# The output projection of a mixer block, split by the rows of its weight: one half computed among the latent projections

## The chip, the cores and the metric

The kernel runs on one core of a Trainium2 chip. The metric is device time in microseconds (us) for one execution of the whole kernel; the kernel before took 1762.07 us, the median of three runs (1761.93 to 1762.74). PE is the matrix engine (TensorE), DVE the vector engine, ACT the scalar engine, POOL the GpSimd engine, and SP the engine on which nearly all loads are issued. SBUF is the on-chip memory, PSUM the accumulators that PE writes.

## The reference, cut to what matters

One layer on a sequence of 1024 tokens with 1024 features, in float32:

```
x = x + 1/2 * SwiGLU_1(RMSNorm(x))
h = RMSNorm(x) @ W_in            -> u (512) | v (512) | c_q (256) | c_kv (128) | k_rope (32)
y_A = gelu(u) * (masked W_s @ RMSNorm(gelu(v)) + b)          # gMLP, 512 wide
q = rmsnorm(c_q) @ w_uq ; k, v = rmsnorm(c_kv) @ w_ukv       # the latents; per-head norms, rotary
y_B = block-causal attention(q, k, v)                         # 8 heads, 512 wide
x = x + concat(RMSNorm(y_A), RMSNorm(y_B)) @ W_out            # W_out is 1024 x 1024
x = x + 1/2 * SwiGLU_2(RMSNorm(x))
x = RMSNorm(x)
```

RMSNorm(y_A) and RMSNorm(y_B) are separate norms, so the product with W_out is a sum of two: the gMLP half times the first 512 rows of W_out, and the attention half times the last 512 rows.

## The kernel before

**Tiles.** The 1024 tokens are eight row tiles t of 128. Every float32 product is made of three matmuls on values that are split into a high and a low part: high times high, high times low, low times high. A split is a copy on ACT (the high part, L291) and a subtraction on DVE (the low part, also L291); for the rows of W_out the copy `woh` is on ACT (L1123) and the subtraction `wol` on POOL (L1124).

**Stages, in the order of time.** FFN 1 with gate and up, then down (0 to 650 us), which leaves x in the DRAM tensor `x1d`; v, u and the gMLP (640 to 762 us); the latents (762 to about 860 us); attention (820 to 1010 us); the way out, that is the product with W_out (1011 to 1112 us); FFN 2 (1112 to 1757 us), whose gate and up products are called GU below.

**What sets the order.** The program is a list of `Step` objects, run in order; `before(lead, fn)` puts a piece of work that many steps ahead of a step, and `do` appends a piece. A string of steps such as "a0 c0 a1 k0 l0" names them. A scheduler then reorders instructions on each engine by its own model, and a planner gives each tile its place in SBUF, so that a tile that takes over the place of another has to wait for the last user of that one. DVE, ACT, POOL and SP each work through their instructions in order.

**The steps that matter.** `a` (`latent_in`) multiplies x by the last 416 columns of W_in; `c` (`latent_T`) transposes its result and splits it into `chl`; `l` (`latent_tile`) makes q, k and v of one row tile (L917 to L926 on PE), then on DVE the squares' sums, an inverse square root by three Newton rounds of three small instructions each (L280 to L282), and two scalings (L955, L956), and on POOL the rotary part (L816 to L820, L958). `x` (`attend`) is one stage of attention on one item, a head and a pair of row tiles: head transposes (`head_T`, L973), scores (L988 to L990), softmax (L992, L994), transposed probabilities (L1017), weighted sums (L1026, L1027), the fold (L1038, L1040). The items are taken heads 0 to 2 first, and five stages of attention lie among the last latents.

**The way out.** `gmlp_pair` makes the normed gMLP half `ya` and stores it in the DRAM tensor `yAd`. The eight 128-row pieces of W_out are loaded and split by `load_out` at the end of attention, two pieces to each of the last four items. `y_tile` loads the gMLP half back, norms the attention half beside it, transposes the eight 128x128 blocks and splits them. `out_tile` runs 48 matmuls of 512 columns (eight pieces, two halves of the columns, three products), adds x1 to the two banks (L1163), stores the sum in `x2d`, and makes the normed and transposed operand of FFN 2 (`xo2.tile`: the norm L305, transposes L300, sums and splits L386 to L408). The first weights of GU (`raw_b`, 512 KB for each load) are loaded at the leads of `load_at`.

Of the kernel before, what the change touches and what calls it, by code (L numbers as in the profile page):

```python
# [11 lines left out]
F32R = mybir.dt.float32r  # L12
# [222 lines left out]
def block(nc, x, positions, ffn1_norm, ffn1_w_gate, ffn1_w_up,  # L235
# [71 lines left out]
    def rows(t):  # L307
        return slice(t * P, (t + 1) * P)
# [328 lines left out]
    yAd = nc.dram([S, GW], "yAd")  # L637
# [248 lines left out]
    def gmlp_pair(p):  # L886
        u, ps = mx["u"][p], mx.pop(("mix", p))
        for g in range(4):
            gs = slice(g * P, (g + 1) * P)
            nc.vector.scalar_tensor_tensor(u[:, :, gs], ps[:, g], bT[:, g:g + 1], u[:, :, gs],  # L890
                                           op0=ALU.add, op1=ALU.mult)
        for j in range(2):
            t = 2 * p + j
            ya = tile_([P, GW], f"ya{t}")
            r = row_rstd(u[:, j, :], ya, f"ya{t}", GW)
            nc.vector.scalar_tensor_tensor(ya, u[:, j, :], r, mx["goA"], op0=ALU.mult, op1=ALU.mult)
            nc.gpsimd.dma_start(yAd[rows(t), :], ya)
# [145 lines left out]
    items = [(h, pi) for ps in ((0, 1), (2, 3)) for h in range(3) for pi in ps]  # L1043
    items += [(h, pi) for h in range(3, H) for pi in range(NT // 2)]
# [5 lines left out]
    def attend(n):  # L1050
# [66 lines left out]
    def load_out(k):
        hi = tile_([P, D], f"woh{k}", F32R)
        lo = tile_([P, D], f"wol{k}", F32R)
        for e in range(2):  # L1120
            es = slice(e * 512, (e + 1) * 512)
            raw = load(tile_([P, 512], f"raw_wo{k}_{e}"), wov[:, k, es])
            nc.scalar.copy(hi[:, es], raw)  # L1123
            nc.gpsimd.tensor_tensor(lo[:, es], raw, f(hi[:, es]), op=ALU.subtract)  # L1124
        wo[k] = (hi, lo)
# [8 lines left out]
    def y_tile(t):  # L1134
        y = tile_([P, D], f"y{t}")
        load(y[:, 0:GW], yAd[rows(t), :])
        ysrc = mx["yB"][t // 4][:, t % 4].rearrange("p h d -> p (h d)")
        r = row_rstd(ysrc, y[:, GW:], f"yb{t}", GW)
        nc.vector.scalar_tensor_tensor(y[:, GW:], ysrc, r, mx["goB"], op0=ALU.mult, op1=ALU.mult)
        hv = transposed(y, f"y{t}")  # L1140
        yh = tile_([P, KD, P], f"yh{t}", F32R)
        yl = tile_([P, KD, P], f"yl{t}", F32R)
        for k in range(2):
            split(hv[k], yh[:, 4 * k:4 * k + 4, :], yl[:, 4 * k:4 * k + 4, :])
        mx["y", t] = (yh, yl)
# [3 lines left out]
    def out_tile(t):  # L1149
        x2 = row_tile(x1d[rows(t), :], f"x2_{t}")  # L1150
        yh, yl = mx["y", t]
        pe = [bank(f"wo{t}_{e}") for e in range(2)]
        for k in range(KD):
            wh, wl = wo[k]
            for e in range(2):
                es = slice(e * 512, (e + 1) * 512)
                mm(pe[e], yh[:, k, :], wh[:, es], start=k == 0, stop=False)  # L1157
                mm(pe[e], yh[:, k, :], wl[:, es], start=False, stop=False)  # L1158
            for e in range(2):
                mm(pe[e], yl[:, k, :], wh[:, e * 512:(e + 1) * 512], start=False, stop=k == KD - 1)  # L1160
        for e in range(2):
            es = slice(e * 512, (e + 1) * 512)
            nc.vector.tensor_tensor(x2[:, es], pe[e], x2[:, es], op=ALU.add)  # L1163
# [8 lines left out]
    for t in range(2, NT):  # L1172
        ws_[t].before(1, lambda t=t: y_tile(t), ws_[0].index)
# [3 lines left out]
    gu2.steps(GU_ORDER, base2 - 1, load_at={(0, 0): base2 - 2, (0, 1): base2 - 1, (1, 0): base2, (1, 1): base2,  # L1177
# [63 lines left out]
```

## Time and profile before

| | us |
|---|---|
| median of three runs | 1762.07 |
| the profiled execution, its own time | 1762.42 |
| its span in the trace | 1760.6 |
| PE busy | 1716.5 (97%) |
| DVE busy | 1132.8 (64%) |
| ACT busy | 740.3 (42%) |
| POOL busy | 151.5 (9%) |
| chain of work that ended last: PE, DVE, ACT, DMA | 90%, 4%, 3%, 2% |

The span is 1.8 us shorter than the profiled execution's own time, and that execution is 0.35 us over the median. Busy PE includes time at the lower clock, so a busy share of 97% does not mean that 97% of the time is needed: the granted clock (1.00 is 2.4 GHz, 0.50 is 1.2 GHz) has to be read beside it. A matmul's printed duration is longer than its share of the engine, since matmuls are pipelined; what one costs is the distance of two starts.

### The profile page before, as it was taken

To read this page: it belongs to the slowest core of one execution; us is meant where nothing else is said; L and a number is where in the kernel's file an instruction comes from. 1 tells how busy PE (TensorE), PEld (TensorE's weight loads), DVE (VectorE), ACT (ScalarE), POOL (GpSimd) and SP (SyncE) were. 2 spreads that over 40 slices of the span, in tenths; PEclk is the share of its full clock that TensorE was granted. 3 is DMA by queue.
4 is the path that set the end of the run, shared out by engine and by line. 5 is a ranking of instruction groups with operands and counts; after the bars stand their busy time and mean duration, and the time that the engine had idled before them with its cause. 6 is when DMAs were issued, how large, how long until landed. Compare 5 with 4: busy or idle time off the path is not lost.

```text
span 1760.6 us, 21281 instructions
## 1 busy us (share of the span) xinstructions
PE 1716.5 (97%) x8196; PEld 1446.7 (82%) x8196; DVE 1132.8 (64%) x1597; ACT 740.3 (42%) x1125; POOL 151.5 (9%) x288
## 2 busy tenths in 40 slices
PE   8999999999999999999799999999999999999997
PEld 7788888888888888898699888778888888888886
DVE  7965656555578567469777644675665555648774
ACT  6533333334324344346577823443333333433442
POOL 1100000000000004333200511000000000000010
PEclk9999999999999999999799999999999999999999
DMA  7043232325835521200000422413322231693431
GB/s 257 12 144 120 90 120 90 112 74 195 313 125 186 167 85 48 94 25 1 1 1 1 158 88 97 161 54 112 127 102 90 96 118 70 210 345 107 161 126 48
DMA packets 122981, 199.51 MB, mean 113 GB/s; under 512 B 11008, under 2 KB 57600, under 8 KB 122880
## 3 DMA queue, kind: packets, MB, share of 16 engines
q1 hardware_dynamic: 118784, 184.52, 31.1%
q0 software_dynamic: 3520, 12.58, 1.8%
q8 instruction: 64, 1.05, 0.2%
q10 hardware_dynamic: 576, 1.05, 0.2%
q14 instruction: 37, 0.30, 0.1%
HBM read 143.07 MB, written 55.05 MB: 113 GB/s over the span
## 4 chain that ended last, share of the span: by engine, by line
PE 90%; DVE 4%; ACT 3%; DMA 2%; issue 1%; POOL 0%; SPq 0%; POOLq 0%; ACTq 0%; DVEq 0%
PE psum L468 46%; PE psum L597 8%; PE psum L599 8%; PE psum L600 8%; PE psum L744 2%; PE psum L745 2%; PE psum L746 2%; PE psum L1160 2%; PE psum L1157 2%; PE psum L1158 2%; PE psum L1017 2%; PE psum L300 1%; PE psum L1027 1%; PE psum L1026 1%; PE psum L988 1%; PE psum L990 1%
## 5 line engine op out<-in xcount | busy, mean ns | idle before, releaser
L483 DVE TENSOR_TENSOR P_a<-psum,P_a 128x1024 f32<-128x1024 f32 x33 | 40.3, 1222 | 80.1 <-PE psum L468 80.1
L483 DVE TENSOR_TENSOR P_b<-psum,P_b 128x1024 f32<-128x1024 f32 x33 | 40.3, 1222 | 59.4 <-PE psum L468 59.4
L473 ACT COPY P_b<-psum 128x1024 f32<-128x1024 f32 x33 | 33.5, 1014 | 77.3 <-PE psum L468 77.3
L473 ACT COPY P_a<-psum 128x1024 f32<-128x1024 f32 x33 | 33.5, 1016 | 73.4 <-PE psum L468 73.4
L484 ACT ACTIVATE P_a<-P_a 128x512 f32<-128x512 f32 x33 | 20.9, 633 | 102.7 <-DVE P_a L483 102.6
L271 POOL TENSOR_TENSOR r_fin<-ms_fin,mhalf 128x1 f32<-128x1 f32 x8 | 7.0, 876 | 610.7 <-DVE ms_fin L269 610.7
L291 DVE TENSOR_TENSOR pl<-psum,ph 128x512 fp32r<-128x512 f32 (+1 forms) x80 | 48.5, 629 | 14.1 <-ACT ph L291 14.1
L992 DVE TENSOR_REDUCE nm<-psum 128x1 f32<-128x128 f32 (+3 forms) x64 | 47.0, 751 | 12.9 <-PE psum L990 12.8
L725 POOL DMA_DIRECT2D x1d<-x_a x8 | 4.6, 580 | 569.9 <-DVE x_a L611 568.3
L994 ACT ACTIVATE p<-psum,nm 128x128 f32<-128x128 f32 (+3 forms) x64 | 47.8, 752 | 12.9 <-DVE nm L992 11.7
L484 ACT ACTIVATE P_b<-P_b 128x512 f32<-128x512 f32 x33 | 20.8, 631 | 76.6 <-DVE P_b L483 76.4
L1157 PE MATMUL psum<-woh,yh 128*128 128x512 f32 x128 | 51.2, 400 | 0.0
L1158 PE MATMUL psum<-wol,yh 128*128 128x512 f32 x128 | 49.9, 390 | 0.0
L1017 PE MATMUL psum<-ident,p 128*128 128x128 f32 x288 | 44.2, 285 | 4.9 <-ACT p L994 4.9
L1027 PE MATMUL psum<-pl,vv 128*128 128x256 f32 x160 | 43.7, 299 | 3.2 <-DVE pl L291 3.2
L1160 PE MATMUL psum<-woh,yl 128*128 128x512 f32 x128 | 45.2, 392 | 0.0
L1026 PE MATMUL psum<-ph,vv 128*128 128x256 f32 x160 | 43.9, 298 | 1.3 <-ACT ph L291 1.3
L291 ACT CAST ph<-psum 128x512 fp32r<-128x512 f32 (+1 forms) x80 | 41.4, 559 | 8.5 <-PE psum L1017 6.6
L988 PE MATMUL psum<-kh,qh 128*128 128x512 f32 (+2 forms) x96 | 38.6, 406 | 3.7 <-ACT kn L940 3.5
L1017 PEld LDWEIGHTS psum<-ident,p 128*128 128x128 f32 x288 | 35.0, 148 | 7.7 <-ACT p L994 5.9
L611 DVE SCALAR_TENSOR_TENSOR x_b<-psum,x_b 128x512 f32<-128x512 f32 x32 | 21.0, 685 | 27.0 <-PE psum L600 27.0
L1027 PEld LDWEIGHTS psum<-pl,vv 128*128 128x128 f32 x160 | 31.3, 196 | 4.9 <-DVE pl L291 3.6
(525 smaller groups left out, 5256.9 us busy)
## 6 DMA issues: line engine op xcount, KB each, us to landing
raw_a<-in_ffn_w_gate SPq DMA_DIRECT2D x22, 512.0 KB, 4.3
raw_a<-in_ffn_w_up SPq DMA_DIRECT2D x22, 512.0 KB, 5.7
hd<-hS_a SPq DMA_DIRECT2D x44, 256.0 KB, 2.2
raw_b<-in_ffn_w_gate SPq DMA_DIRECT2D x22, 512.0 KB, 4.1
raw_b<-in_ffn_w_up SPq DMA_DIRECT2D x22, 512.0 KB, 5.1
hd<-hS_b SPq DMA_DIRECT2D x44, 256.0 KB, 2.2
wB_a<-in_ffn_w_down SPq DMA_DIRECT2D x20, 512.0 KB, 5.3
aS_a<-hd SPq DMA_DIRECT2D x20, 512.0 KB, 3.7
```

The source lines that it names most:

```text
L291: return nc.scalar.copy(hi, src), nc.vector.tensor_tensor(lo, src, f(hi), op=ALU.subtract)
L468: mm(bk[:, m * 512:(m + 1) * 512], lhs[:, 4 * m + k, :], rhs[:, k, :], start=pn in FIRST and n == k == 0, stop=n == 2 and k == 3, skip_gro ...
L473: nc.scalar.copy(ev[u, pn], bk)
L483: nc.vector.tensor_tensor(c, bk, c, op=ALU.add)
L597: mm(banks[t], hh[:, j, tl], dh[:, j, :], start=pn in DOWN_FIRST and c == 0 and j == 0, stop=False, skip_group_check=True)
L599: mm(banks[t], hh[:, j, tl], dl[:, j, :], start=False, stop=False, skip_group_check=True)
L600: mm(banks[t], hl[:, j, tl], dh[:, j, :], start=False, stop=c == 5, skip_group_check=True)
L1017: nc.tensor.transpose(ps[:, i * P:(i + 1) * P], prs[j][:, c * P:(c + 1) * P], ident)
L1027: mm(acc[:, 0:256], mx["vv"][c][:, h, :], lo, start=False, stop=i == len(pts) - 1)
L1157: mm(pe[e], yh[:, k, :], wh[:, es], start=k == 0, stop=False)
L1158: mm(pe[e], yh[:, k, :], wl[:, es], start=False, stop=False)
L1160: mm(pe[e], yl[:, k, :], wh[:, e * 512:(e + 1) * 512], start=False, stop=k == KD - 1)
```

## The change

**What it does.** The product with W_out is taken apart by rows. `out_half(t, half, src)` multiplies one half: 24 matmuls (four pieces of W_out, two column halves, three products), and adds `src` to the banks. The gMLP half of row tile t is a step `o` of its own (`out_a`), which adds x1 and stores the sum in a new DRAM tensor `x15d`; its transposes and split (`y_a`) come one step ahead. The eight steps o0 to o7 stand among the steps l4 to l7 and the first three stages of attention. `ya` stays in SBUF until it is transposed there, so `yAd` with its eight stores and loads is gone. Four pieces of W_out are loaded and split eight, six, four and two steps ahead of o0, the other four at the last two items of attention. `out_tile` computes the attention half alone and adds `x15d`, not x1.

**What else moves with it.** The steps `a` come earlier and the steps `l` later. Three stages of attention lie among the latents, not five; the first items are those of heads 0 and 1 only, and the transposes of head 2 are made where those of the other heads are. `y_tile(t)` runs two steps ahead of its `out_tile`, not one, and the first weights of GU are due one to two steps earlier, in steps that are now half as long.

```diff
-            nc.gpsimd.dma_start(yAd[rows(t), :], ya)
+            mx["ya", t] = ya
...
-    items = [(h, pi) for ps in ((0, 1), (2, 3)) for h in range(3) for pi in ps]
-    items += [(h, pi) for h in range(3, H) for pi in range(NT // 2)]
+    items = [(h, pi) for ps in ((0, 1), (2, 3)) for h in range(2) for pi in ps]
+    items += [(h, pi) for h in range(2, H) for pi in range(NT // 2)]
...
-        if n == 2:
-            st.do(lambda: head_T(2, 0))
-        if n == 5:
+        if n == 3:
             st.do(lambda: head_T(0, 1))
             st.do(lambda: head_T(1, 1))
...
-                if op == "T" and n == 8:
-                    st.do(lambda: head_T(2, 1))
-                if op == "T" and 1 < h < H - 1 and pi in TP:
+                if op == "T" and 0 < h < H - 1 and pi in TP:
...
+    def y_transposed(y, t, half):
+
+        ps = bank(f"ty{half}{t}")
+        for k in range(4):
+            nc.tensor.transpose(ps[:, k * P:(k + 1) * P], y[:, k * P:(k + 1) * P], ident)
+        yhl = tile_([P, 2, 4, P], f"yhl{half}{t}", F32R)
+        split(ps.rearrange("p (k t) -> p k t", k=4), yhl[:, 0], yhl[:, 1])
+        return yhl
+
+    def out_half(t, half, src):
+
+        xt = row_tile(src[rows(t), :], f"x{half}_{t}")
+        yhl = mx.pop(("yhl", half, t))
+        pe = [bank(f"wo{half}{t}_{e}") for e in range(2)]
+        for n, (i, j) in enumerate(((0, 0), (0, 1), (1, 0))):
+            for e in range(2):
+                for k in range(4):
+                    mm(pe[e], yhl[:, i, k, :], wo[4 * half + k][j][:, e * 512:(e + 1) * 512], start=n == k == 0,
+                       stop=n == 2 and k == 3)
+        for e in range(2):
+            es = slice(e * 512, (e + 1) * 512)
+            nc.vector.tensor_tensor(xt[:, es], pe[e], xt[:, es], op=ALU.add)
+        return xt
+
+    def out_a(t):
+        xt = out_half(t, 0, x1d)
+        nc.gpsimd.dma_start(x15d[rows(t), :], xt)
...
-    for ch in ("u0 u1 m0 g0 u2 u3 m1 g1 u4 u5 m2 g2 u6 u7 m3 g3 a0 c0 a1 k0 l0 c1 a2 l1 c2 a3 k1 l2 c3 a4 l3 c4 a5 k2 l4 "
-               "c5 a6 c6 a7 l5 c7 k3 x0 l6 x1 l7 x2 x3 x4").split():
+    for ch in ("u0 u1 m0 g0 u2 u3 m1 g1 u4 u5 m2 g2 u6 u7 m3 g3 a0 c0 a1 k0 l0 c1 a2 a3 k1 l1 c2 a4 a5 k2 l2 c3 a6 a7 k3 l3 c4 "
+               "o0 l4 c5 o1 l5 c6 o2 l6 c7 o3 l7 o4 x0 o5 o6 x1 o7 x2").split():
...
+    for t in range(NT):
+        sm[f"o{t}"].before(1, lambda t=t: y_a(t))
+    for k in range(4):
+        sm["o0"].before(8 - 2 * k, lambda k=k: load_out(k))
...
-    for k in range(KD):
-        att[last - 3 + k // 2].before(0, lambda k=k: load_out(k))
+    for k in range(4):
+        att[last - 2 + k // 2].before(0, lambda k=k: load_out(4 + k))
...
     def out_tile(t):
-        x2 = row_tile(x1d[rows(t), :], f"x2_{t}")
...
+        x2 = out_half(t, 1, x15d)
...
-        ws_[t].before(1, lambda t=t: y_tile(t), ws_[0].index)
+        ws_[t].before(2, lambda t=t: y_tile(t), ws_[0].index)
...
-    gu2.steps(GU_ORDER, base2 - 1, load_at={(0, 0): base2 - 2, (0, 1): base2 - 1, (1, 0): base2, (1, 1): base2,
+    gu2.steps(GU_ORDER, base2 - 1, load_at={(0, 0): base2 - 4, (0, 1): base2 - 3, (1, 0): base2 - 2, (1, 1): base2 - 1,
                                              (2, 0): base2, (2, 1): base2})
```

**What stands where.** First PE, among the last latents, of before: the last products of one latent tile (L924 to L926), the transposes of the next `chl` (L903), the transposes of head 0 for the row tiles 0 to 3 (L973, `qn` and `kn`), and the products of the next latent tile (L917, L918).

```order
1930 L924 MATMUL psum<-wkv_h,chl_7355 128x512
1931 L925 MATMUL psum<-wkv_l,chl_7355 128x512
1932 L926 MATMUL psum<-wkv_h,chl_7355 128x512
1933 L903 MATMUL psum<-ident,at_6515 128x128 x3
1934 L973 MATMUL psum<-ident,qn_6783 128x128
1935 L973 MATMUL psum<-ident,qn_6906 128x128
1936 L973 MATMUL psum<-ident,qn_7040 128x128
1937 L973 MATMUL psum<-ident,qn_7165 128x128
1938 L903 MATMUL psum<-ident,at_6515 128x128 x3
1939 L917 MATMUL psum<-wuq0h,chl_7409 128x384
1940 L918 MATMUL psum<-wuq0l,chl_7409 128x384
1941 L973 MATMUL psum<-ident,kn_6785 128x128
```

The same place of the kernel after the change, with the matmuls of `out_half` (L1104) and the transposes of `ya` (L1091); the four transposes of `qn` stood fifty rows ahead.

```order
2086 L917 MATMUL psum<-wuq1h,chl_7786 128x384
2087 L918 MATMUL psum<-wuq1l,chl_7786 128x384
2088 L919 MATMUL psum<-wuq1h,chl_7786 128x384
2089 L973 MATMUL psum<-ident,kn_6773 128x128
2090 L973 MATMUL psum<-ident,kn_6951 128x128
2091 L973 MATMUL psum<-ident,kn_7144 128x128
2092 L973 MATMUL psum<-ident,kn_7366 128x128
2093 L1091 MATMUL psum<-ident,ya_6608 128x128 x4
2094 L1104 MATMUL psum<-woh_7102,yhl_7937 128x512
2095 L1104 MATMUL psum<-woh_7196,yhl_7937 128x512
2096 L1104 MATMUL psum<-woh_7263,yhl_7937 128x512
2097 L1104 MATMUL psum<-woh_7329,yhl_7937 128x512
```

The transposes of the heads, which need finished q and k, now stand behind whole groups of out matmuls and not right behind the latent products.

Next DVE, among the last latents, of before: the end of the Newton rounds of one latent tile (`t_qk`, `r_qk`), and the maxima, splits and scalings around it.

```order
768 L282 SCALAR_TENSOR_TENSOR r_qk_7506<-t_qk_7507,r_qk_7506 128x16
769 L978 SCALAR_TENSOR_TENSOR ql_7779<-psum,gqcol,qh_7776 128x512
770 L280 TENSOR_TENSOR t_qk_7507<-r_qk_7506 128x16
771 L992 TENSOR_REDUCE nm_3_7691<-psum 128x1
772 L281 SCALAR_TENSOR_TENSOR t_qk_7507<-t_qk_7507,ssq_7487 128x16
```

The same kind of place after the change, where `yhl` is the split of a transposed half and `x_1` the row tile to which the out product is added (L1108).

```order
735 L281 SCALAR_TENSOR_TENSOR t_qk_7509<-t_qk_7509,ssq_7490 128x16
736 L291 TENSOR_TENSOR yhl_7659<-psum,yhl_7659 128x512
737 L282 SCALAR_TENSOR_TENSOR r_qk_7508<-t_qk_7509,r_qk_7508 128x16
738 L1108 TENSOR_TENSOR x_1_7551<-psum,x_1_7551 128x512 x2
739 L280 TENSOR_TENSOR t_qk_7509<-r_qk_7508 128x16
```

Splits and adds of the out product now stand inside the Newton rounds, where attention's instructions stood.

Last SP, at the end of the way out, of before: the loads of x1 (`x_6`, `x_7`) and of the first GU weights.

```order
257 L311 DMA x_6_10962<-x1d 128x1024
258 L311 DMA raw_b_10958<-in_ffn_w_gate 128x4x256
259 L311 DMA raw_b_10958<-in_ffn_w_up 128x4x256
260 L311 DMA raw_b_11040<-in_ffn_w_gate 128x4x256
261 L311 DMA raw_b_11040<-in_ffn_w_up 128x4x256
262 L311 DMA raw_b_11153<-in_ffn_w_gate 128x4x256
263 L311 DMA raw_b_11153<-in_ffn_w_up 128x4x256
264 L311 DMA raw_b_11158<-in_ffn_w_gate 128x4x256
265 L311 DMA raw_b_11141<-in_ffn_w_gate 128x4x256
266 L311 DMA raw_b_11141<-in_ffn_w_up 128x4x256
267 L311 DMA raw_b_11158<-in_ffn_w_up 128x4x256
268 L311 DMA x_7_11051<-x1d 128x1024
```

The same place after the change.

```order
255 L311 DMA x_4_10916<-x15d 128x1024
256 L311 DMA raw_b_10912<-in_ffn_w_gate 128x4x256
257 L311 DMA raw_b_10912<-in_ffn_w_up 128x4x256
258 L311 DMA x_5_11003<-x15d 128x1024
259 L311 DMA raw_b_10998<-in_ffn_w_gate 128x4x256
260 L311 DMA raw_b_10998<-in_ffn_w_up 128x4x256
261 L311 DMA x_6_11060<-x15d 128x1024
262 L311 DMA raw_b_11055<-in_ffn_w_gate 128x4x256
263 L311 DMA raw_b_11055<-in_ffn_w_up 128x4x256
264 L311 DMA x_7_11123<-x15d 128x1024
```

The first pair of weights now stands ahead of the load of row tile 5 and no longer behind that of row tile 6, and the last row tile is loaded between the pairs.

## Rows read from the trace of the kernel before

**Rows 1.** The page: the chain that ended last, by engine and share of the span

```profile
PE 90%; DVE 4%; ACT 3%; DMA 2%; issue 1%; POOL 0%; SPq 0%; POOLq 0%; ACTq 0%; DVEq 0%
```

**Rows 2.** Windows: length; busy us of PE, PEld, DVE, ACT, POOL; clock; DMA share, GB/s

```profile
800.00:820.00 20.00, 18.99 (x106) 17.70 (x104) 19.62 (x78) 13.85 (x35) 9.62 (x20) 1.00 0.01 2
820.00:840.00 20.00, 15.42 (x82) 14.18 (x82) 16.28 (x46) 13.64 (x27) 5.24 (x12) 0.83 0.00 1
840.00:860.00 20.00, 12.58 (x46) 9.95 (x46) 15.70 (x50) 6.89 (x21) 7.34 (x14) 0.55 0.00 0
860.00:880.00 20.00, 18.61 (x117) 17.19 (x118) 13.47 (x26) 13.03 (x29) 2.71 (x12) 0.86 0.01 2
...
980.00:1000.00 20.00, 16.61 (x114) 15.49 (x113) 11.53 (x25) 17.97 (x42) 19.25 (x21) 0.91 0.43 141
...
1060.00:1100.00 40.00, 40.00 (x205) 33.61 (x203) 20.38 (x34) 14.04 (x29) 5.05 (x9) 1.00 0.31 106
...
1120.00:1140.00 20.00, 16.57 (x71) 13.32 (x70) 14.92 (x16) 10.02 (x13) 1.14 (x2) 0.91 0.32 115
1140.00:1160.00 20.00, 18.07 (x79) 14.65 (x78) 16.23 (x16) 10.55 (x13) 0.00 (x0) 0.98 0.04 14
1160.00:1180.00 20.00, 20.00 (x83) 16.36 (x83) 16.82 (x16) 9.30 (x10) 0.00 (x0) 0.93 0.07 26
```

**Rows 3.** Windows of 5 us among the last latents, columns as above

```profile
815.00:820.00 5.00, 3.99 (x24) 3.12 (x22) 5.00 (x35) 4.57 (x14) 2.79 (x9) 1.00 0.00 0
820.00:825.00 5.00, 1.87 (x7) 1.88 (x8) 5.00 (x14) 1.91 (x3) 2.48 (x4) 0.63 0.00 0
...
845.00:850.00 5.00, 3.38 (x13) 2.17 (x12) 4.26 (x9) 1.06 (x2) 2.89 (x5) 0.50 0.00 0
```

**Rows 4.** Waits of PE, 815 to 870 us: total us, times, longest us

```profile
PE psum L973 <- DVE chl L291: 3.8, 1, 3.8
PE psum L988 <- ACT kn L940: 3.5, 1, 3.5
PE psum L1027 <- DVE pl L291: 3.0, 2, 2.6
```

**Rows 5.** Timeline of PE in the way out: start us, duration us, instruction

```profile
1040.44 0.60 PE L300 MATMUL psum<-ident,y 128*128 128x128 f32 x4
1040.79 0.48 PE L1157 MATMUL psum<-woh,yh 128*128 128x512 f32 x1
...
1041.34 0.40 PE L1160 MATMUL psum<-woh,yl 128*128 128x512 f32 x1
...
1042.73 0.40 PE L1160 MATMUL psum<-woh,yl 128*128 128x512 f32 x1
```

**Rows 6.** A line of DVE, 780 to 870 us: count, busy us, mean ns, idle before

```profile
L282 DVE SCALAR_TENSOR_TENSOR r_qk<-t_qk,r_qk 128x16 f32<-128x16 f32 x24 | 4.1, 172 | 0.3
```

**Rows 7.** End of attention: a wait of PE, ACT and POOL lines (960 to 1010 us)

```profile
984.78 1.84 PE L1017 MATMUL psum<-ident,p 128*128 128x128 f32 x9 [3.21 <-ACT p L994]
...
L1124 POOL TENSOR_TENSOR wol<-raw_wo,woh 128x512 fp32r<-128x512 f32 x16 | 20.2, 1312 | 1.7 <-ACT woh L1123 1.7
...
L1123 ACT CAST woh<-raw_wo 128x512 fp32r<-128x512 f32 x16 | 9.5, 645 | 0.8 <-DMA raw_wo<-in_w_out 0.8
```

**Rows 8.** Lines of DVE in the way out, 1011 to 1112 us

```profile
L291 DVE TENSOR_TENSOR yl<-psum,yh 128x512 fp32r<-128x512 f32 x15 | 10.2, 683 | 4.8 <-ACT yh L291 4.8
L1163 DVE TENSOR_TENSOR x<-psum,x 128x512 f32<-128x512 f32 x14 | 9.1, 685 | 6.6 <-PE psum L1160 5.6 <-DMA x<-x1d 1.1
L305 DVE SCALAR_TENSOR_TENSOR xn_f<-x,r_f,g 128x1024 f32<-128x1024 f32 x7 | 9.0, 1285 | 5.2 <-POOL r_f L271 5.2
```

**Rows 9.** Start of FFN 2: waits of PE (1108 to 1200 us), one piece of the chain

```profile
PE psum L468 <- ACT A11h_b L455: 3.4, 1, 3.4
PE psum L468 <- DVE P_b L483: 1.9, 1, 1.9
...
1115.52 10.38 DMA raw_b<-in_ffn_w_up
```

More of the change, by code (lines that the diff above doesn't have):

```diff
@@ L636, in block @@
     x2d = nc.dram([S, D], "x2d")
-    yAd = nc.dram([S, GW], "yAd")
+    x15d = nc.dram([S, D], "x15d")
     hds = [nc.dram([7 * NU * P, 512], f"hd{i}") for i in range(2)]
@@ L1076, in attend, with load_out @@
                 st.do(lambda i=items[n - D1]: weighted(*i))
+    wov = w_out[0].rearrange("(k p) e -> p k e", p=P)
+    wo = {}
+    def load_out(k):
+        hi = tile_([P, D], f"woh{k}", F32R)
+        lo = tile_([P, D], f"wol{k}", F32R)
+        for e in range(2):
+            es = slice(e * 512, (e + 1) * 512)
+            raw = load(tile_([P, 512], f"raw_wo{k}_{e}"), wov[:, k, es])
+            nc.scalar.copy(hi[:, es], raw)
+            nc.gpsimd.tensor_tensor(lo[:, es], raw, f(hi[:, es]), op=ALU.subtract)
+        wo[k] = (hi, lo)
@@ new lines, in y_transposed @@
+    def y_transposed(y, t, half):
[14 more added lines that the diff above has]
+                       stop=n == 2 and k == 3)
+        for e in range(2):
+            es = slice(e * 512, (e + 1) * 512)
+            nc.vector.tensor_tensor(xt[:, es], pe[e], xt[:, es], op=ALU.add)
+        return xt
@@ L1079, in block, with y_a @@
+    def out_a(t):
+        xt = out_half(t, 0, x1d)
+        nc.gpsimd.dma_start(x15d[rows(t), :], xt)
+    def y_a(t):
+        mx["yhl", 0, t] = y_transposed(mx.pop(("ya", t)), t, 0)
     vs = [Step(lambda t=t: v_tile(t)) for t in range(NT)]
     sm = {}
-    works = {"u": u_tile, "m": mix_pair, "g": gmlp_pair, "a": latent_in, "k": key_rope, "c": latent_T, "l": latent_tile}
-    for ch in ("u0 u1 m0 g0 u2 u3 m1 g1 u4 u5 m2 g2 u6 u7 m3 g3 a0 c0 a1 k0 l0 c1 a2 l1 c2 a3 k1 l2 c3 a4 l3 c4 a5 k2 l4 "
-               "c5 a6 c6 a7 l5 c7 k3 x0 l6 x1 l7 x2 x3 x4").split():
+    works = {"u": u_tile, "m": mix_pair, "g": gmlp_pair, "a": latent_in, "k": key_rope, "c": latent_T, "l": latent_tile, "o": out_a}
@@ L1112, in block @@
         attend(n)
-    wov = w_out[0].rearrange("(k p) e -> p k e", p=P)
-    wo = {}
     last = len(items) - 1
[L1117 to L1125, printed above, removed]
-    for k in range(KD):
-        att[last - 3 + k // 2].before(0, lambda k=k: load_out(k))
+    for k in range(4):
+        att[last - 2 + k // 2].before(0, lambda k=k: load_out(4 + k))
     def out_gain_b():
@@ L1134, in y_tile @@
     def y_tile(t):
-        y = tile_([P, D], f"y{t}")
-        load(y[:, 0:GW], yAd[rows(t), :])
+        y = tile_([P, GW], f"y{t}")
         ysrc = mx["yB"][t // 4][:, t % 4].rearrange("p h d -> p (h d)")
[L1138 to L1145, printed above, removed]
+        r = row_rstd(ysrc, y, f"yb{t}", GW)
+        nc.vector.scalar_tensor_tensor(y, ysrc, r, mx["goB"], op0=ALU.mult, op1=ALU.mult)
+        mx["yhl", 1, t] = y_transposed(y, t, 1)
     xo2 = XOps("f2")
     def out_tile(t):
-        x2 = row_tile(x1d[rows(t), :], f"x2_{t}")
[L1151 to L1163, printed above, removed]
+        x2 = out_half(t, 1, x15d)
         nc.gpsimd.dma_start(x2d[rows(t), :], x2)
```

## The prediction

> **What bounds the kernel now.** First the page: the chain that ended last is PE for 90% [rows 1], so only time that PE gives away can be won. The windows tell where it does, and there two columns are to be read together: PE's busy time, and the clock granted to it. What a stretch gives away is its idle time plus its busy time times what the clock lacks of 1.00. From 800 to 880 us PE idles 1.01 + 4.58 + 7.42 + 1.39 = 14.4 us, and the clock takes 15.42 x 0.17 + 12.58 x 0.45 + 18.61 x 0.14 = 10.9 us: 25.3 us in all. From 980 to 1000 us it is 3.4 + 1.5 = 4.9 us, from 1120 to 1180 us 3.43 + 1.93 + 1.5 + 0.4 + 1.4 = 8.7 us [rows 2]. The way out in between is full: 40 of 40 us at 1.00. So there are three holes, 38.9 us together, on either side of work that has none.
>
> Then what makes each hole. In the first, DVE is busy 5.00 of 5 us twice while PE falls to 3.99 and 1.87, and from then on PE runs in pieces at 0.63 and later 0.50 [rows 3]; the long waits are for `chl` on DVE (3.8 us), for `kn` on ACT (3.5) and for the low part of the probabilities on DVE (3.0) [rows 4]. It is a chain and not a load: each of the last latents goes through nine small DVE instructions in a row (24 of one of the three kinds in this stretch, 172 ns each) [rows 6], and then through POOL, and PE has nothing else to do. In the second, ACT is busy 17.97 of 20 us and makes the sixteen copies of W_out (645 ns each) between the exponentials, for one of which PE waits 3.21 us [rows 2, 7]. In the third, GU's first weights are issued behind the last out matmuls and land 10.38 us later; PE waits 3.4 us for their copy [rows 9].
>
> **The change part by part.** The sum is made against the profiled execution, 1762.4 us, 0.35 us over the median.
>
> *Moved out matmuls.* Out of the way out go 8 x 24 = 192 matmuls and 8 x 4 = 32 transposes. Starts of six matmuls lie (1042.73 - 1041.34)/6 = 0.23 us apart, four transposes take 0.35 us [rows 5]: 192 x 0.23 + 8 x 0.35 = 44.2 + 2.8 = 47.0 us of PE at full clock. The same 47.0 us appear among the latents. As work this is neutral; the gain is what of the first hole they fill. The filling is ample (47.0 against 25.3), so its amount does not limit; its place and the other engines do.
>
> DVE gets there 8 splits and 16 adds, 8 x 0.683 + 16 x 0.685 = 16.4 us [rows 8], ACT eight copies of `yhl` and eight of W_out, about 8 x 0.6 + 8 x 0.645 = 10 us, POOL eight `wol`, 8 x 1.312 = 10.5 us [rows 7]. From 800 to 880 us DVE is busy 65.1 of 80 us [rows 2]. With 16.4 us more it needs 81.5 us; PE needs 80 - 25.3 + 47.0 = 101.7 us. DVE's share becomes 80%, about what it is: it does not bound by its load, it can by its order.
>
> Four things, by the order of the instructions, keep the hole from closing. (1) The first out group needs the last pieces of W_out, whose loads take over places of tiles of the third latent tile, and a split that stands on DVE behind that tile's chain; no row shows this wait. Bounds 0 and 3.8 us, the wait for `chl` [rows 4], the nearest; I take 3. (2) The chain of the last latent is as long as before, and only one out group and the first scores stand ahead of what needs it. Bounds 0 and 3.5 + 3.0 = 6.5 us, the waits for `kn` and `pl` there now [rows 4]; I take 4, since the work in front has grown but DVE's list has too. (3) On SP the x1 of tile 3 takes the place of that of tile 1, so it waits for that one's store, and the x1 of tile 2 stands behind it; DVE's add waits for it and all the chain behind that. Bounds 0 and 3.8 us by the same row (nothing nearer); I take 2. (4) Clock: with 9 of 14.4 us of idle time left in shorter pieces I take 4 of the 10.9 us. Left over: 3 + 4 + 2 + 4 = 13. **First hole: -12 us**, bounds -25 (none of the four) and +0 (3.8 + 6.5 + 3.8 + 10.9 = 25.0).
>
> On point 4 the rows show that the clock was at 1.00 with PE busy 3.99 of 5 us, fell to 0.63 with 1.87 of 5, and was 0.50 with 3.38 of 5 [rows 3]: once down, it stayed down among short waits. The Trainium skill, page "TensorE: Matmul & The Clock Gate", section "HAM oscillation — how this bites in real kernels", says that a loop with a recurring wait pays for the fall of the clock at every turn. By that the three waits left would keep all of the 10.9 us, and the sum of this part would be -5 and not -12; by the rows the fall began with a single wait of 3.8 us, and the waits that I leave are mostly shorter.
>
> *Half the copies of W_out.* Eight of sixteen leave the end of attention: 8 x 0.645 = 5.2 us of ACT's 17.97 [rows 2, 7]. The hole of 4.9 us came from ACT alone. Bounds 0 and -4.9; **-3 us**, since the four pieces still come at the last two items. Two stages of attention and the transposes of head 2 move behind the latents; as PE work they are neutral, and hidden as the rest of attention is (20 of 20 us busy around it).
>
> *DRAM.* Eight stores and loads of 256 KB go, eight of each of 512 KB come. The path is store, then load many steps later, and the way out shows no wait for a load above the 1.1 us in front of the adds [rows 8]. I cost it at nothing; if that cover is gone, 1.1 us.
>
> *Way out.* A tile now takes 24 x 0.23 + 12 transposes x 0.09 = 6.6 us of PE. On DVE a tile took 20.38 x 12.7/40 = 6.5 us (12.7 us being 48 x 0.23 + 16 x 0.1 us) and loses one split of 0.68 [rows 2, 8]: 5.8 us, or 88% of PE's 6.6. DVE was at half load here, and now is as full as in the third hole (81%, 84%). There PE lost 8.7 of 60 us, though half of it to the late load. Against that, GU's first weights are issued between the loads of the row tiles, some 20 us ahead, and the 3.4 us and the clock behind them (1.5) should go. Bounds: -8.7 (the hole gone, nothing new) and +13 (DVE waits in each of eight tiles as it now waits for others, 4.8 + 6.6 + 5.2 us over seven tiles, 2.4 each [rows 8], on top of its 5.8: 8.2 us, 1.6 over PE's 6.6). I take **-2 us**: 5 won at the weights, 3 lost to DVE.
>
> Sum: -12 - 3 - 2 = -17; 1762.4 - 17 = **1745.4 us**, relative to the median about 1745.
>
> **The rivals.** *All is filled.* The chain has enough in front of it, and DVE keeps up: -22 - 4 - 6 gives 1730. For it speaks that PE needs 101.7 us and DVE 81.5; against it points 1 to 3, which are in the order of the instructions.
>
> *New waits for old ones.* The out groups wait for DVE in the order in which it works, the clock stays low in between, and of the 25.3 us only 3 to 5 come back: 1762 - 4 - 1 = 1757. For it speaks that DVE was busy 5.00 of 5 us when PE first ran dry [rows 3], and that adds now stand inside the Newton rounds.
>
> *Slower: the halved way out is DVE's.* If on DVE every tile costs its work of 5.8 us plus the 2.4 us in which it now waits for others and that PE's long tile hid, the stretch goes at 8.2 us per tile and not 6.6, and the six splits of GU's first weights come on top (an estimate: twice as wide as the 0.683 us split [rows 8], 1.3 us each, 7.8 us together): 13 + 7 = 20 us lost there. With -12 - 3 elsewhere that is +5: 1767. It decides from a tile of 8.6 us with no splits in the way: (8.6 - 6.6) x 8 = 16, the gain of the rest. Against it: most of those waits are for a PE that now comes sooner, and y is made two tiles ahead.
>
> *It does not do what it says.* W_out's pieces or x1 come so late on SP's one list that the out groups run behind the latents: the holes stay, 1762 to 1765. Little speaks for it, since the DMA engines are idle there (share 0.00 to 0.01) [rows 2].
>
> **How the numbers follow.** Forecast (1738 to 1752) 0.50; all filled 0.13; new waits 0.20, of which 0.13 is faster by over 0.2% (3.5 us, about what a measurement of this kernel can tell from no change); DVE's way out 0.12, all slower; the last 0.05, of which 0.02 is no change. Faster 0.50 + 0.13 + 0.13 = 0.76; same 0.07 + 0.02 = 0.09; slower 0.12 + 0.03 = 0.15. The range 1729 to 1766 leaves out half of the first rival and most of the third.
>
> **What would show it.** Right: from 800 us to the end of the latents PE idles under 10 us and the clock stays near 1.00; the last tiles of the way out lie 6.6 to 7.2 us apart; no wait for `A11h_b`; ACT under 15 of 20 us late in attention. Wrong: clock windows of 0.50 among the latents again; a PE wait for `yhl` or for `woh`; way out tiles over 8 us apart with DVE above 95%; an add that waits for a load of x1.

## The result and the profile after

The changed kernel took 1747.97 us (median of four runs, 1745.66 to 1749.61), the kernel before 1762.40 us beside it (1761.93 to 1765.33). The ratio is 0.9914, with a 95% interval of 0.9896 to 0.9931: faster by 0.7 to 1.0%. The forecast was 1745, with a range of 1729 to 1766. The profiled execution took 1746.63 us, 15.8 less than that of before.

First the page of the changed kernel: busy time and share of the span, then the chain by engine.

```profile
PE 1707.9 (98%) x8196; PEld 1437.1 (82%) x8196; DVE 1143.1 (66%) x1613; ACT 739.9 (42%) x1125; POOL 154.7 (9%) x288
...
PE 90%; DVE 3%; ACT 3%; DMA 2%; issue 1%; POOL 1%; SPq 0%; POOLq 0%; ACTq 0%; DVEq 0%
```

PE is what ends last, as before [rows 1], and its busy time fell by 8.6 us, although it has the same 8196 instructions: fewer of them ran at the low clock. DVE has the sixteen adds more. Where the time went is in the windows of the changed kernel, which like all windows below are those of one execution (length; busy us of PE, PEld, DVE, ACT, POOL; clock; DMA share, GB/s).

```profile
800.00:820.00 20.00, 18.28 (x97) 15.72 (x95) 15.72 (x81) 11.78 (x36) 10.61 (x16) 1.00 0.19 56
820.00:840.00 20.00, 18.40 (x84) 15.73 (x85) 14.31 (x40) 9.69 (x18) 7.54 (x15) 0.91 0.24 79
840.00:860.00 20.00, 18.73 (x87) 14.91 (x86) 16.29 (x38) 6.36 (x11) 8.66 (x15) 1.00 0.46 159
860.00:880.00 20.00, 20.00 (x113) 17.53 (x112) 18.12 (x51) 10.10 (x21) 6.04 (x13) 1.00 0.19 78
880.00:900.00 20.00, 19.29 (x121) 16.90 (x119) 13.95 (x27) 11.49 (x28) 5.07 (x14) 1.00 0.21 80
...
1000.00:1020.00 20.00, 17.87 (x133) 16.37 (x132) 13.75 (x29) 16.81 (x39) 9.65 (x18) 1.00 0.47 145
...
1040.00:1060.00 20.00, 17.72 (x90) 14.84 (x89) 12.12 (x22) 7.50 (x16) 3.71 (x7) 0.93 0.52 161
1060.00:1080.00 20.00, 16.90 (x88) 13.81 (x87) 11.80 (x20) 9.35 (x20) 3.37 (x6) 0.98 0.46 149
1080.00:1100.00 20.00, 17.28 (x82) 13.99 (x81) 12.56 (x20) 8.71 (x16) 2.82 (x5) 0.91 0.76 244
1100.00:1120.00 20.00, 20.00 (x98) 16.74 (x97) 14.78 (x20) 9.13 (x14) 2.27 (x4) 1.00 0.36 126
...
1140.00:1160.00 20.00, 19.88 (x88) 16.16 (x87) 17.06 (x16) 11.46 (x14) 0.00 (x0) 1.00 0.03 13
```

Read as before, idle time plus busy time times what the clock lacks:

- Among the latents (800 to 900 us): 1.72 + 1.60 + 1.27 + 0.71 = 5.3 us idle and 18.40 x 0.09 = 1.7 us of clock, 7.0 us, where it was 25.3 [rows 2]. **-18.3 us.**
- Late attention (1000 to 1020 us): 2.1 us idle and no clock, where it was 4.9 from 980 to 1000 [rows 2]. Small pieces elsewhere in attention add up to much the same in both kernels. **About -2 us.**
- The way out (1040 to 1100 us): 2.28 + 3.10 + 2.72 = 8.1 us idle and 1.24 + 0.34 + 1.56 = 3.1 us of clock, where it was full [rows 2]. **+11.2 us.** This hole is new.
- Start of FFN 2 (1100 to 1180 us): 0.1 us, where it was 8.7 [rows 2]. **-8.6 us.**

Together -17.7, of which the execution shows -15.8; the 1.9 us between them are not accounted for. Of the waits of PE in the first hole (total us, times, longest) these are left, in the changed kernel from 800 to 900 us, where it was one of 3.8, one of 3.5 and 3.0 in two [rows 4]:

```profile
PE psum L1104 <- DVE x L1108: 3.0, 2, 2.0
PE psum L917 <- ACT kn L940: 1.3, 1, 1.3
PE psum L1027 <- DVE pl L291: 0.6, 1, 0.6
```

And these make the new hole, from 1036 to 1110 us:

```profile
PE psum L1104 <- ACT b_f L376: 5.4, 3, 2.3
PE psum L1104 <- ACT yhl L291: 2.4, 1, 2.4
PE psum L300 <- DVE xn_f L305: 0.3, 1, 0.3
```

Out matmuls (L1104) wait for a copy on ACT (`b_f`, L376) whose value they do not use: it is the copy of the transposed, normed row tile for FFN 2. What they wait for is its PSUM bank, as the run with the copy first bears out below. PE's and then ACT's timeline in the changed kernel show why the copy is late (start us, duration us): PE starts the transposes at 1071.88 us, and the waiting matmuls at 1075.65.

```profile
1071.88 1.03 PE L300 MATMUL psum<-ident,xn_f 128*128 128x128 f32 x8
...
1075.65 1.20 PE L1104 MATMUL psum<-woh,yhl 128*128 128x512 f32 x4 [2.30 <-ACT b_f L376]
```

```profile
1072.51 0.59 ACT L291 CAST xB11h_f<-psum 128x512 fp32r<-128x512 f32 x1 [3.97 <-PE psum L300]
1072.99 1.06 ACT L287 ACTIVATE xn_f<-x 128x1024 f32<-128x1024 f32 x1
...
1074.05 0.57 ACT L291 CAST xB21h_f<-psum 128x512 fp32r<-128x512 f32 x1
1074.51 0.60 ACT L291 CAST yhl<-psum 128x512 fp32r<-128x512 f32 x1
1074.99 0.61 ACT L376 COPY b_f<-psum 128x512 f32<-128x512 f32 x1
1075.46 0.66 ACT L287 ACTIVATE y<-yB 128x512 f32<-128x512 f32 x1
...
1076.09 0.60 ACT L376 COPY b_f<-psum 128x512 f32<-128x512 f32 x1
```

Two banks hold the transposed tile. Each is read by a cast and a subtraction (the split) and by the copy, and ACT takes the square of the next row tile, a cast of `yhl` and the square of `y` in between. So the first copy ends 3.7 us after the transposes began and the second 4.8 us after. In the kernel before, both ended 3.2 us after the transposes of a row tile began (at 1046.37 us):

```profile
1048.44 1.11 ACT L376 COPY b_f<-psum 128x512 f32<-128x512 f32 x2
```

In a tile of 12.7 us that hid; in one of 6.6 it does not.

### The profile page after: what moved, and what is told of

Read it like the earlier page. It is cut to its first block, busy times and chain, and to the rows that moved or that the text cites. A ratio compares the mean times of both kernels' runs of the same rounds, so it can differ in the third digit from the quotient of the medians.

```text
span 1744.8 us, 21298 instructions
## 1 busy us (share of the span) xinstructions
PE 1707.9 (98%) x8196; PEld 1437.1 (82%) x8196; DVE 1143.1 (66%) x1613; ACT 739.9 (42%) x1125; POOL 154.7 (9%) x288
## 4 chain that ended last, share of the span: by engine, by line
PE 90%; DVE 3%; ACT 3%; DMA 2%; issue 1%; POOL 1%; SPq 0%; POOLq 0%; ACTq 0%; DVEq 0%
PE psum L468 47%; PE psum L597 8%; PE psum L600 8%; PE psum L599 8%; PE psum L1104 3%; PE psum L746 2%; PE psum L744 2%; PE psum L745 2%; PE psum L1017 2%; PE psum L1027 1%; PE psum L1026 1%; PE psum L988 1%; PE psum L990 1%; PE psum L989 1%; PE psum L300 1%
## 5 line engine op out<-in xcount | busy, mean ns | idle before, releaser
L1104 PE MATMUL psum<-woh,yhl 128*128 128x512 f32 x256 | 71.7, 410 | 11.1 <-ACT b_f L376 5.4
L1104 PEld LDWEIGHTS psum<-woh,yhl 128*128 128x128 f32 x256 | 48.4, 195 | 23.2 <-ACT b_f L376 6.3
L994 ACT ACTIVATE p<-psum,nm 128x128 f32<-128x128 f32 (+4 forms) x64 | 47.7, 750 | 13.0 <-DVE nm L992 7.5
L1104 PE MATMUL psum<-wol,yhl 128*128 128x512 f32 x128 | 35.7, 402 | 0.0
L456 DVE TENSOR_TENSOR A12l_b<-raw_b,A12h_b 128x1024 fp32r<-128x1024 f32 x11 | 13.4, 1222 | 31.1 <-ACT A12h_b L455 20.7
```

What stands on the lines that cost most here:

```text
L1104: mm(pe[e], yhl[:, i, k, :], wo[4 * half + k][j][:, e * 512:(e + 1) * 512], start=n == k == 0, stop=n == 2 and k == 3)
```

## The experiments

Each run is against the kernel before on the same chip. For the comparison with the changed kernel, note that its ratio is 0.9914.

**Is the filling the gain?** The out steps of the gMLP half go behind the last item of attention, all else stays.

```diff
-               "o0 l4 c5 o1 l5 c6 o2 l6 c7 o3 l7 o4 x0 o5 o6 x1 o7 x2").split():
+               "l4 c5 l5 c6 l6 c7 l7 x0 x1 x2").split():
...
     last = len(items) - 1
+    for t in range(NT):
+        sm[f"o{t}"] = Step(lambda t=t: out_a(t))
```

> The changed kernel, but the eight out steps of the gMLP half run behind the last item of attention and no longer among the latents; the split by rows, the new order of latents and items and the early weights of GU stay. Theory (filling the latents' hole is worth 18 us, by idle time and clock of 800 to 900 us before and after): that hole opens again, 1747 + 18 = about 1765. Rival (the gain comes from the new order of latents and items and from the early weights): within 5 us of the changed kernel, 1742 to 1752.

Measured: 1770.87 us, ratio 1.0051 (1.0036 to 1.0066). That is slower than before and 23 us above the changed kernel. Its windows and its longest waits of PE from 800 to 880 us:

```profile
820.00:840.00 20.00, 14.34 (x82) 12.81 (x82) 18.86 (x51) 13.54 (x25) 6.09 (x13) 0.99 0.00 1
840.00:860.00 20.00, 11.81 (x50) 9.29 (x50) 19.38 (x52) 10.21 (x25) 9.16 (x18) 0.75 0.00 1
860.00:880.00 20.00, 13.59 (x68) 11.64 (x68) 13.37 (x33) 8.69 (x19) 3.95 (x10) 0.74 0.00 0
```

```profile
PE psum L924 <- ACT kn L940: 5.8, 2, 4.6
PE psum L973 <- DVE ri L1035: 4.6, 1, 4.6
PE psum L988 <- ACT kn L940: 4.4, 1, 4.4
```

The hole is back: with 1.1 us of idle time from 800 to 820 it is 21.4 us idle and 6.6 of clock, 28 us, 21 more than in the changed kernel. So 21 of the 23 us are the hole, and the filling is the gain. That this run is also slower than the kernel before does not come from the halved way out: from 1040 to 1180 us it loses 7.7 us, where the kernel before lost 8.7 at the start of FFN 2. It comes mostly from a wait of 3.5 us for a weight in FFN 1 (`wT2l_a`), with 1.5 us of clock behind it, from 540 to 560 us, far ahead of the edit; neither kernel has it. Without those 5 us it would be at about 1766, where the theory put it.

**What does the moved work cost where it now stands?** The gMLP half is left out (transposes, splits, weights, matmuls).

```diff
     def out_a(t):
-        xt = out_half(t, 0, x1d)
+        xt = row_tile(x1d[rows(t), :], f"x0_{t}")
```

> The changed kernel without the gMLP half of the output product: its four weight pieces, transposes, splits and 192 matmuls are left out, x1 is loaded and stored as it is. Theory (of the 47 us of moved PE work 18 lie in time that PE had idle or at the low clock): 47 - 18 = 29 us less, about 1718, with the first hole open again. Rival (the added DVE, ACT and POOL work lengthens the chain of the latents, and its cost is hidden in the net gain): clearly under 1712. Second rival (the work is wholly covered): over 1735.

Measured: 1717.68 us, ratio 0.9749 (0.9734 to 0.9764), 30.3 us under the changed kernel. So work of 47.0 us of PE costs 30 us. The hole is open again:

```profile
840.00:860.00 20.00, 8.76 (x28) 6.31 (x27) 19.07 (x57) 7.53 (x16) 7.96 (x14) 0.59 0.07 27
```

From 800 to 880 us it is 22.4 us idle and 7.9 of clock, 30.3 us, where the changed kernel has 7.0: the moved work fills 23 us and not 18, since the new order without it leaves more than the kernel before. That the run is shorter by 30 us and not by 47 - 23 = 24 comes mostly from its way out, which loses 6.6 us and not 11.2. So the theory's 29 us were met partly by luck. Both rivals' times are missed, by 6 and by 17 us.

**What holds the way out?** In `XOps.tile`, for FFN 2 alone and its row tiles 0 to 3, the transposed tile is copied out of PSUM first, and the split is made from the copy.

```diff
+            if self.nm == "f2":
+                for key, v in zip(("B11", "B21"), hv):
+                    self.keep(key, v, cs)
+                for key in ("B11", "B21"):
+                    self.cut(key, self.b[key][:, :, cs], cs)
+                return
```

> The changed kernel; in the way out, the transposed normed row tiles 0 to 3 are copied out of PSUM first (b_f, L376), and the split is then made from that copy, so that a bank is free after one ACT instruction. Theory (the 11 us that the halved way out loses are waits for PSUM banks that ACT's late copies hold): the waits on b_f (5.4 us) and the clock behind them go, 1747 - 5 to 9 = 1738 to 1742. Rival (DVE's 5.8 us per tile is the bound of the way out): another wait takes the place, 1745 to 1749.

Measured: **1734.08 us**, ratio 0.9845 (0.9830 to 0.9859), 14 us under the changed kernel (the profiled executions: 12.5) and more than expected. Windows of the way out, and ACT's timeline at one row tile, of this run (the copy is L382 here):

```profile
1040.00:1060.00 20.00, 19.98 (x110) 16.83 (x108) 11.89 (x22) 7.99 (x17) 3.39 (x6) 1.00 0.50 161
1060.00:1080.00 20.00, 19.54 (x98) 16.19 (x99) 14.33 (x25) 11.96 (x27) 4.75 (x9) 1.00 0.58 192
1080.00:1100.00 20.00, 20.00 (x103) 16.77 (x102) 17.24 (x25) 11.47 (x17) 3.70 (x7) 1.00 0.82 269
```

```profile
1073.79 1.07 ACT L382 COPY b_f<-psum 128x512 f32<-128x512 f32 x2 [2.61 <-PE psum L300]
1074.75 1.07 ACT L287 ACTIVATE xn_f<-x 128x1024 f32<-128x1024 f32 x1
...
1075.80 0.62 ACT L291 CAST xB11h_f<-b_f 128x512 fp32r<-128x512 f32 x1
1076.31 0.63 ACT L291 CAST xB21h_f<-b_f 128x512 fp32r<-128x512 f32 x1
```

Both copies are done 1.07 us after they start, before anything else, and 1.7 us after the transposes began (1073.16); the idle time of the way out falls from 8.1 to 0.5 us, and the clock is 1.00. Every engine runs as many instructions as in the changed kernel, and DVE and ACT are as busy (1141.0 and 739.8 us over the span, there 1143.1 and 739.9). The bank was the bound, and neither DVE nor ACT by its load. The way out gives 10.7 us of the gain; some 2 us more come from the latents, where the same waits stand but the clock did not fall this time. This run beats both kernels.

The same edit on the kernel before:

> The kernel before with the copy out of PSUM first, as in the run that won 14 us on the changed kernel. Theory (the PSUM waits exist only because a halved row tile needs its banks again after 6.6 us and not 12.7): no gain, 1760 to 1764. Rival (the old order of copies was a cost in both kernels): 1748 to 1757.

Measured: 1760.86 us, ratio 0.9988 (0.9977 to 0.9999): under 0.25%, no gain of that kind. The order of the copies was free while a row tile took 12.7 us; the change made it dear.

**Why did the hole at the start of FFN 2 close?** Three runs: the changed kernel with the old leads, the kernel before with an earlier lead, and the changed kernel with four high parts of W_out kept to the end. With three of the leads a step earlier the kernel before has no room in SBUF for its tiles and gave no time, so only one was moved.

```diff
-load_at={(0, 0): base2 - 4, (0, 1): base2 - 3, (1, 0): base2 - 2, (1, 1): base2 - 1,
+load_at={(0, 0): base2 - 2, (0, 1): base2 - 1, (1, 0): base2, (1, 1): base2,
```

> The changed kernel with the old leads for GU's first weights (the first due two steps ahead, not four; in steps half as long). Theory (the hole of 8.7 us at the start of FFN 2 closed because the weights land before they are needed): part of it comes back, PE waits for A11h or A12h again, 1747 + 3 to 8 = 1750 to 1755. Rival (SP's list waits for tiles to come free anyway, whatever the lead): no change, 1745 to 1749.

Measured: 1746.49 us, ratio 0.9916 (0.9899 to 0.9932): no change in the time. The first two pairs are issued as early as in the changed kernel (1051.5 and 1071.0 us, there 1053.9 and 1073.4), but the third at 1092.1 us, where it was 1082.8, and half of the hole is back:

```profile
1140.00:1160.00 20.00, 16.77 (x68) 13.39 (x67) 17.23 (x16) 11.59 (x12) 0.00 (x0) 0.91 0.03 13
```

```profile
PE psum L468 <- ACT S3h_b L455: 3.2, 1, 3.2
```

That is 3.2 us idle and 1.5 of clock, behind the copy of a sum of weights (`S3h_b`). So the theory holds by the trace in its size, though the copy is another one, and only the time looks like the rival's: in this execution the way out lost 9.2 us and not 11.2, and among the latents the clock did not fall (1.7 us).

```diff
-load_at={(0, 0): base2 - 2,
+load_at={(0, 0): base2 - 3,
```

> The kernel before with only GU's very first weights due one row tile (12.7 us) earlier. Theory (places in SBUF, not the lead, set when these loads start): 1760 to 1764, first pair issued within 3 us of where it was, 1095 us. Rival (the lead): pair issued some 12 us earlier and 1755 to 1759.

Measured: 1756.93 us, ratio 0.9971 (0.9961 to 0.9981). The theory fell: the lead alone wins 5 us in the kernel before. SP's issue of the first weights in the kernel before, and then in this run:

```profile
1095.40 0.38 SPq L311 DMA_DIRECT2D raw_b<-in_ffn_w_gate  x1
```

```profile
1085.71 0.38 SPq L311 DMA_DIRECT2D raw_b<-in_ffn_w_gate  x1
```

PE's wait of 3.4 us for `A11h_b` is gone, and of the hole's 5.4 us of idle time 2.5 are left (waits for P_b, 1.4 and 1.1). It was not the first pair that PE had waited for. In the kernel before, the copy that ended the wait (started at 1125.98 us) was of a load that SP issued last, at 1115.52, behind that of row tile 7; with the first pair out of the way the loads behind it moved up on SP's list, and the same copy (the third of `A11h_b`) starts at 1121.89 us.

```diff
+        if t == NT - 1:
+            for k in range(4):
+                for j in range(1):
+                    nc.gpsimd.tensor_copy(small(f"hold{k}{j}"), f(wo[k][j][:, 0:1]))
```

> The changed kernel; the high parts of the first four pieces of W_out (16 KB of each partition) are kept to the end of the way out by a read of one column of each. Theory (the hole at the start of FFN 2 closed because the places of these pieces are free for GU's weights): the third to sixth pair of weights is issued later and PE waits for their copies again, 1747 + 2 to 7 = 1749 to 1754. Rival (it closed because the order of the loads changed): 1745 to 1748, and the pairs issued as in the changed kernel.

Measured: 1750.36 us, ratio 0.9927 (0.9910 to 0.9945). By time this is not settled, since the interval overlaps that of the changed kernel. By the trace, the first two pairs are as early as there (1055.8 and 1074.7 us), the next three 6 to 11 us later (1093.6, 1101.6, 1102.7, where it was 1082.8, 1091.8, 1096.5), and 3.9 us of idle time are back from 1140 to 1160 us, with 1.4 of clock; PE waits there for `P_b` (2.6 and 1.2 us) and not for a copy of the weights. SP's waits give two reasons: the third pair stands behind three loads of row tiles on the list, where it stood behind one, and before the fourth SP waits 6.9 us for out matmuls. So in this run and in that with the old leads a third pair some 10 us later goes with some 5 us of the hole. The lead counts, as both kernels show; that free places count too is likely, but this run changed the order of the list with them.

**Is the new order of items part of it?** The changed kernel with heads 0 to 2 first.

```diff
-    items = [(h, pi) for ps in ((0, 1), (2, 3)) for h in range(2) for pi in ps]
+    items = [(h, pi) for ps in ((0, 1), (2, 3)) for h in range(3) for pi in ps]
```

> The changed kernel with attention's items in the old order (heads 0 to 2 first, transposes of head 2 among the latents). Theory (the gain among the latents is the filling alone): 1744 to 1751. Rival (the new order of items is part of it): 1752 or more.

Measured: 1767.16 us, ratio 1.0021 (1.0012 to 1.0031): 19 us lost. By its number the rival holds: from 780 to 900 us this run loses 22.4 us idle and 7.6 of clock, 30.0 us, with the out steps in their place. The kernel before, with the old order and without them, lost 25.3, the new order without them 28.0 (the out steps behind attention), both together 7.0. So the filling wins only in the new order. The trace gives another reason than a lack of work. PE waited once for 10.3 us for the first `yhl`. ACT's copy, and what POOL did ahead of it, in this run:

```profile
825.32 0.58 ACT L291 CAST yhl<-psum 128x512 fp32r<-128x512 f32 x1 [6.72 <-POOL late L820]
```

```profile
814.82 4.97 POOL L1088 TENSOR_TENSOR wol<-raw_wo,woh 128x512 fp32r<-128x512 f32 x4 [3.07 <-ACT woh L1087]
```

The copy takes its value from PSUM and none from `late`, the rotary key; it was held by POOL's list, on which four low parts of W_out (4.97 us) stood ahead of `late`. The likely reason is a place in SBUF that the one takes over from the other; the trace shows the wait and not the place.

**Can what is left among the latents be won?** To the run with the copy first, x1's loads four steps ahead and W_out's pieces six steps earlier; and x1's loads alone.

```diff
-        sm["o0"].before(8 - 2 * k, lambda k=k: load_out(k))
+        sm["o0"].before(14 - 2 * k, lambda k=k: load_out(k))
...
+        sm[f"o{t}"].before(4, lambda t=t: mx.__setitem__(("xa", t), row_tile(x1d[rows(t), :], f"x0_{t}")))
```

> The run with the copy first (1734 us), and besides x1's row tiles loaded four steps ahead of their out step and the first four pieces of W_out six steps earlier. Theory (the waits that are left among the latents, 3.0 us for adds of the out product, come from x1's loads and W_out's, which stand in the chain with 6.8 us and 7.0 us): 1728 to 1732. Rival (they come from DVE's order; tiles that live longer push others out): 1733 or more.

Measured: 1745.77 us, ratio 0.9900 (0.9882 to 0.9919), 12 us worse than the copy alone. The 3.0 us of waits for the adds are gone, but PE now waits 6.5 us for `yhl` among the latents (3.7 at once).

> The run with the copy first (1734 us), and besides only x1's row tiles loaded four steps ahead of their out step; W_out's pieces as there. It tells apart which half of the run that took both lost 12 us. Theory (the loss came from W_out's pieces, which live six steps longer and take the places of the latents' tiles): 1730 to 1736. Rival (it came from x1's tiles, 4 KB each): 1740 or more.

Measured: 1764.72 us, ratio 1.0015 (1.0005 to 1.0025), 31 us worse: more than with W_out's pieces moved as well, so neither half explains the other. PE waited 14.9 us at once for a `chl`, whose copy on ACT was held:

```profile
828.00 0.48 ACT L291 CAST chl<-psum 128x384 fp32r<-128x384 f32 x1 [9.68 <-DVE rl L282]
```

Again the copy takes no value of `rl`; DVE was in the Newton rounds of other tiles. Loads that were asked for earlier removed a wait and made larger ones. Why, and whether a taken-over place in SBUF is behind it, stays open.

**Late attention.** To the run with the copy first, W_out's last four pieces spread over four items.

```diff
-        att[last - 2 + k // 2].before(0, lambda k=k: load_out(4 + k))
+        att[last - 4 + k].before(0, lambda k=k: load_out(4 + k))
```

> The run with the copy first (1734 us), with the last four pieces of W_out at one each of the last five items but one, not two each at the last two full ones. Theory (the 2.4 us that PE idles near 1010 us are ACT's eight copies between exponentials): 1731 to 1734. Rival (the pieces' longer life pushes other tiles, as x1's and W_out's did among the latents): 1736 or more.

Measured: 1734.32 us, ratio 0.9840 (0.9824 to 0.9856): no change. From 1000 to 1020 us PE now idles 0.6 us and not 2.35, but from 880 to 900 us it idles 2.2 and not 0.7.

## Why the prediction was right, and where it was not

The sign and the main mechanism were right: 1745 forecast, 1748 measured. That the sum was so close is partly luck. The two gains came out 9.9 us larger than forecast and the loss on the way out 8.2 us larger, and these errors cancel.

| term | forecast | by the windows |
|---|---|---|
| latents filled | -12 | -18.3 |
| half the copies of W_out | -3 | about -2 |
| way out halved | +3 | +11.2 |
| first weights of GU earlier | -5 | -8.6 |
| sum | -17 | -17.7 (execution: -15.8) |

*Latents.* The mechanism held: with the out steps taken away (1771 us) the hole is there, with them it closes to 7 us. It needed the new order of items as well, which the sum did not ask about. The four things that were to keep it from closing were over-sized: 13 us forecast, 7.0 found. The first out group (point 1, 3 us taken) started without a wait. What PE waited for instead were DVE's adds of the out product (2.0 and 1.0 us), likely for the banks of the out group before; only the rival of new waits had these. The last latents (point 2, 4 us) left 1.3 us for `kn` and 0.6 for `pl`. DVE's wait for x1 (point 3, 2 us) was 0.9 us, and no wait of PE is put down to it. On point 4, the clock fell once, to 0.91, and took 1.7 us, not 4. The rule that was weighed there (the Trainium skill, "TensorE: Matmul & The Clock Gate", section "HAM oscillation — how this bites in real kernels") would have kept all 10.9 us if long waits had stayed; here they did not stay, so this run does not test it. In the run without the gMLP half, where they did, the granted clock was 0.93, 0.84, 0.59 and 0.96 over the four windows from 800 to 880 us (1.00, 0.83, 0.55 and 0.86 in the kernel before) and took 7.9 us.

*Way out.* This is the step that failed. "DVE was at half load here, and now is as full as in the third hole" named the wrong engine and the wrong kind of bound. DVE is busy 11.8 to 12.6 of 20 us there, not 88%, and PE waits mostly for ACT, which is busy 7.5 to 9.4. With the copy first DVE rises to 17.24 of 20 us (86%), and PE loses nothing in that window. The prediction counted work per engine and per tile, and did not count how long a PSUM bank stays taken. The bound of +13 for this term held, but it was made of other waits, those of DVE. What was left out is visible in the trace of before, though in none of the rows: out matmuls, `y` and `xn` transposes all need banks, and the copy L376 stands behind other work on ACT. The rival of a DVE-bound way out (1767) is refuted as to its cause by the run with the copy first. (In its sum 7.8 us were entered as 7; with 7.8 it gives 1768.)

*First weights.* The size was missed since the whole hole went, not just the wait for `A11h_b`: idle time 5.4 us and the clock behind it. The reading of the hole was wrong in one point: the first weights were not issued behind the last out matmuls but at 1095.40 us, and the load that landed 10.38 us later, for whose copy PE waited, was the last of six pairs. And 5 us of the gain did not need the change at all; one number in the kernel before gives them.

*Late attention.* ACT is busy 16.8 of 20 us from 1000 to 1020, where under 15 was forecast: half as many copies, but packed into one window.

*What the text said would show it.* Idle time among the latents under 10 us, the clock there near 1.00 and no wait for `A11h_b`: right. Row tiles 6.6 to 7.2 us apart: wrong, the transposes of `xn` lie 10.5, 8.3, 6.6 and 12.3 us apart (from 1053.07 to 1090.75). With the copy first they lie 6.9, 7.4, 6.9 and 7.3 apart (from 1052.06 to 1080.48), about as forecast. Of the signs of being wrong three came in part: tiles over 8 us apart, but with DVE at 60% and not above 95%; a PE wait for `yhl` (2.4 us, in the way out); and an add that waited 0.9 us for a load of x1.

## What to carry to other kernels

Where one stage is bound by a chain and the next by work, move independent work of the second into the first, and size it by what the first stage loses in idle time and clock together. The place counts as much as the amount: here the same work in the old order of items closed nothing. Then look at what the shortened stage did in the shadow of the work that left: a step of half the length needs its PSUM banks back in half the time, so the first thing that touches a bank should be the one that empties it. A load asked for earlier is not free: for GU's first weights it won 5 us, for x1 and W_out among the latents it cost 12 and 31 us. A likely reason is that its tile takes over a place in SBUF sooner, but no run here shows the place.

## What was not expected of the hardware

The clock fell also behind waits of some 2 us, but not behind all of them. The way out of the changed kernel has three, of 2.28 us (up to 1056.84), 2.30 (up to 1075.65) and 2.41 (up to 1094.63). Windows of 4 us behind each:

```profile
1056.00:1060.00 4.00, 3.16 (x8) 2.53 (x9) 2.71 (x5) 1.89 (x5) 1.11 (x2) 0.66 1.02 316
...
1076.00:1080.00 4.00, 4.00 (x23) 3.41 (x22) 2.88 (x6) 1.55 (x5) 0.55 (x1) 1.00 0.84 278
...
1096.00:1100.00 4.00, 3.69 (x17) 3.22 (x17) 3.90 (x7) 1.47 (x3) 0.00 (x0) 0.72 0.74 224
```

The same wait of 2.0 us among the latents, for an add of the out product, was followed by a fall in the changed kernel and by none in the run with the copy first:

```profile
820.00:824.00 4.00, 3.65 (x11) 2.88 (x12) 1.56 (x4) 2.14 (x5) 3.09 (x7) 0.72 0.26 105
```

```profile
820.00:824.00 4.00, 2.50 (x11) 2.08 (x12) 2.42 (x5) 0.99 (x3) 3.68 (x7) 1.00 0.01 2
```

In the way out the clock took 3.1 us on top of 8.1 us of idle time, while 2.1 us of idle time in pieces of at most 1.1 us (1000 to 1020 us) left it at 1.00. A single wait of some 2 us can thus cost more than it looks, or not; what decides it is not shown here. So a difference of one or two microseconds between single executions need not come from the edit.
